# Low parts of weights by an accumulating SBUF-to-SBUF transfer instead of a VectorE subtraction

## The chip, the cores and the metric

The kernel runs on one core of a Trainium2 chip. The metric is device time in microseconds for one execution of the whole program, lower is better. The core has a matrix engine (PE, with its weight loads shown as PEld), a vector engine (DVE), a scalar engine (ACT), GpSimd (POOL), and a queue engine for transfers (SP). Each engine runs its own instructions in order and waits on semaphores that others raise. Transfers are issued from the queues of SP, ACT and POOL and carried by the core's 16 DMA engines; those of POOL are the ones that can add into their destination.

## The reference

One layer of a hybrid decoder trunk on a sequence of 2048 tokens with model width 1024, all in float32:

```python
mem_n = rmsnorm(mem, mem_norm_g)                       # 256 memory tokens
h = rmsnorm(x, mix_norm_g)
q, k, v, g, u = split(h @ w_in, [512, 1024, 1536, 2048])
y_ret = silu(g) * head_rmsnorm(retention(q, k, v, positions), ret_gn_g)   # 4 heads of 128
y_pool = pool_mixer(u, pool_w, pool_scale)             # 4 groups, windows 2, 4, 8, 16
x = x + concat([y_ret, y_pool]) @ w_out
x = x + cross_attn(rmsnorm(x, xa_norm_g), mem_n, xa_wq, xa_wkv, xa_wo)    # 4 heads of 256
x = x + conv_glu_ffn(rmsnorm(x, ffn_norm_g), w_up, conv_w, conv_b, w_down)  # hidden 2816
return rmsnorm(x, final_norm_g)
```

## The kernel before

**Numbers as pairs.** Every matrix product is made in three passes. A float32 operand is split into a high part, rounded to the matrix engine's fast format (`F32R`), and a low part, the rest. `passes` (L241 to L243) adds high by high, high by low and low by high into one PSUM bank. `split` (L230) makes a pair: ACT copies the source to the high part, rounding it (L233), and DVE subtracts the high part from the source to give the low part (a line of `tt`, L216). With a scale `g` the two lines are L236 (ACT) and L225 (DVE, through `stt`). The first two passes need only the weight's high part; the third, L243, is the first that reads its low part.

**Tiles and buffers.** The sequence is worked in two blocks of T = 1024 tokens, each in two halves of SUB = 512. Activations stand with features on the 128 partitions. `X` holds the pairs of the eight normed input tiles. `R` is five raw weight buffers of 128x1024 floats; `Q` is three buffers for pairs of 128x512. `Z` and `T` are work space for tiles of 1024 and 512. The tile framework gives each engine an order of its instructions by its own model of their times, and puts in the waits: a buffer is written again only when its last reader is done.

**A unit.** `unit` (L285) makes one 128x1024 tile of output features: SP loads 128x1024 weights into a raw buffer (`load_tile`, L305), `pairs` splits the two halves into two of the three pair buffers, and PE runs 24 matmuls for each half, 12 for each half of the tokens. Per block there are 12 units for the retention heads, 4 for the pooling groups (two of block 1's stand before its heads), 8 for the output projection (`wout_r` and `WPd`, loaded by L1536 and L1537) and 8 for the attention's output (`VWd`): 32, and 64 in all. A raw buffer goes back to SP when both its low parts are made.

**Around the units.** Before the first block, `folded_weights` multiplies the attention's matrices into `Md` (query by key) and `VWd` (value by output); its units of work go on between those of block 0's heads, and its splits are not touched by the change. `attention` (L822) loads `Md` in two halves by two head pairs: `load_m(0)` before its loop, `load_m(1)` during the first eight of its sixteen steps, one 128x1024 raw load (L835) and two splits each; the second half goes to a `Z` buffer. In the attention output of block 0 each unit is followed by `load_x` for block 1: two loads of x (L524), then ACT's L236 and a square (L355), DVE's L225 and a sum. SP's order there is: raw weights of five units on, then loads for the weight sums, then the two x tiles.

**POOL.** In the first 940 us POOL does two things. `weight_sums` forms sums of blocks of the feed-forward weights in DRAM (`Ud`, `Dd`): for each of 34 jobs SP loads four blocks (L913), and POOL adds others to them by accumulating transfers, two at once (L915, L916), then one that needs the first (L919), then one that needs the second (L922). The jobs are stepped between the quarters of a unit. `pool_group` has POOL copy 16 columns of halo (L630, L631) for each half of each group. Later come sums for the feed-forward stage (`sums_of`) and some of its low parts.

**Feed-forward.** From about 1190 us `run` works through `w_up` and `w_dn` in rounds with an order written out in the kernel; it has splits of its own (`Member`, `combining`) that the change leaves alone.

Of the kernel before, what the change touches and what calls it, by code (L numbers as in the profile page):

```python
# [8 lines left out]
F32 = mybir.dt.float32  # L9
F32R = mybir.dt.float32r  # L10
I32 = mybir.dt.int32
AF = mybir.ActivationFunctionType
ALU = mybir.AluOpType
# [8 lines left out]
SUB = 512  # L22
# [97 lines left out]
def trunk(ctx, tc, xT, memT, pos, w_qkgu, w_v, wkv, wqT, wo, wout_r, wout_p, poolT, w_up, w_dn, vecs, consts, outT):  # L120
    nc = tc.nc
    pe, act, dve, pool, sp = nc.tensor, nc.scalar, nc.vector, nc.gpsimd, nc.sync
# [15 lines left out]
    def new_z(dtype):  # L138
        return Arena(cp.tile([P, 8 * T + 4 * EDGE], dtype, tag="Z", name=nm("Z")), 0, 8, T)
# [58 lines left out]
    def mmps():  # L198
        return mmp.tile([P, SUB], F32, tag="mm", name=nm("mm"))
# [6 lines left out]
    def aux():  # L206
        if both[0] and next(turns_) % 3 == 2:
            return single()
        return auxp.tile([P, SUB], F32, tag="aux", name=nm("aux"))

    def small(n=4):
        t = smp.tile([P, 8], F32, tag="sm", name=nm("sm"))
        return t[:, :n]

    def tt(eng, out, a, b, op):
        return eng.tensor_tensor(out=out, in0=a, in1=b, op=op)  # L216

    def ts(eng, out, a, s1, op0, s2=None, op1=None):
        if op1 is None:
            eng.tensor_scalar(out=out, in0=a, scalar1=s1, scalar2=None, op0=op0)  # L220
        else:
            eng.tensor_scalar(out=out, in0=a, scalar1=s1, scalar2=s2, op0=op0, op1=op1)

    def stt(out, a, s, b, op0=ALU.mult, op1=ALU.add):
        dve.scalar_tensor_tensor(out=out, in0=a, scalar=s, in1=b, op0=op0, op1=op1)  # L225
# [4 lines left out]
    def split(src, hi, lo, g=None):  # L230

        if g is None:
            act.activation(hi, src, AF.Copy)  # L233
            tt(dve, lo, src, hi.bitcast(F32), ALU.subtract)
        else:
            act.activation(hi, src, AF.Identity, scale=g)  # L236
            stt(lo, src, g, hi.bitcast(F32), ALU.mult, ALU.subtract)

    def passes(ps, lhs, rhs, start, stop, more=False):
        (lh, ll), (rh, rl) = lhs, rhs  # L240
        pe.matmul(ps, lh, rh, start=start, stop=False, skip_group_check=more)  # L241
        pe.matmul(ps, lh, rl, start=False, stop=False, skip_group_check=more)  # L242
        pe.matmul(ps, ll, rh, start=False, stop=stop, skip_group_check=more)  # L243

    def new_raw():
        r = raws.take()
        r.free()
        return r.f

    def new_pair():  # L250
        r = prs.take()
        r.free()
        return r.r.rearrange("p (i n) -> p i n", i=2)

    def pairs(raw):

        out = []
        for h in range(2):
            r = raw[h] if isinstance(raw, list) else raw[:, h * SUB : (h + 1) * SUB]
            pr = new_pair()  # L260
            split(r, pr[:, 0], pr[:, 1])
            out.append(pr)
        return out

# [20 lines left out]
    def unit(raw, rhs, evac, order=range(4)):  # L285


        hs = pairs(raw)
        ps = [mmps() for _ in range(NS)]
        for h in range(2):  # L290
            for s in range(NS):
                for j, kk in enumerate(order):
                    k = 4 * h + kk
                    w = [hs[h][:, i, kk * P : (kk + 1) * P] for i in range(2)]
                    passes(ps[s], w, rhs(k, s), h + j == 0, h == 1 and j == 3)
                next(behind[0], None)
                quarter[0] += 1
                if not slow[0] or quarter[0] % 2:
                    next(under[0], None)
                if h == 1:  # L300
                    evac(s, ps[s])
# [520 lines left out]
    def attention(sums, beside, pace):  # L822


        scl, nscl = (smp.tile([P, 8], F32, tag="scl", name=nm("scl"), bufs=2) for _ in range(2))
        room = B.take(2 * KT)
        third = [Region(B, room.first + KT * i, KT) for i in range(2)] + [new_z(F32R).take(KT)]
        prob = [third[1], third[0]]

        def load_m(hp):  # L830

            out = mw[hp]
            for kp in range(KT // 2):
                raw = new_raw()
                fetched[0] = sp.dma_start(raw.rearrange("p (k n) -> p k n", k=2), Md[hp, 2 * kp : 2 * kp + 2].rearrange("k p n -> p k n"))  # L835
                if hp == 0 and kp == 0:

                    out += [(pr[:, 0], pr[:, 1]) for pr in pairs(raw)]
                    yield
                    continue  # L840
                for i in range(2):
                    u = third[2 * hp].r[:, (2 * kp + i) * T : (2 * kp + i + 1) * T]
                    split(raw[:, i * SUB : (i + 1) * SUB], u[:, :SUB], u[:, SUB:])
                    out.append((u[:, :SUB], u[:, SUB:]))
                yield

        def turn(pt, t, e):
            tp = aux()
            for j in range(4):
                pe.transpose(tp[:, j * P : (j + 1) * P], e.f[:, j * P : (j + 1) * P], ident)  # L850
            pt4 = pt.r.rearrange("p (i k t) -> p i k t", i=2, t=T)[:, :, :, t * P : (t + 1) * P]
            split(tp.rearrange("p (k t) -> p k t", k=4), pt4[:, 0], pt4[:, 1])
            e.free()

        mw = [[], []]
        for _ in load_m(0):
            pass
        more_m = load_m(1)
        late = []
        for i in range(2 * KT):  # L860
            hp, t = divmod(i, KT)
            ps = mmps()
            for k in range(KT):
                x2 = [X[:, 2 * k + j, t * P : (t + 1) * P] for j in range(2)]
                passes(ps, x2, mw[hp][k], k == 0, k == KT - 1)
            if i == 0:
                rn, _, _ = norm_tables(sums, wide=False)
                ts(dve, scl, rn, 1.0 / 16.0, ALU.mult)
                ts(dve, nscl, rn, -1.0 / 16.0, ALU.mult)
            mx, sm = small(2), small(2)  # L870
            dve.reduce_max(out=mx, in_=ps.rearrange("p (h m) -> p h m", h=2), axis=AX.X)
            ts(dve, mx, mx, nscl[:, t : t + 1], ALU.mult)
            e = TT.take()
            for j in range(2):
                act.activation(e.f[:, j * NMEM : (j + 1) * NMEM], ps[:, j * NMEM : (j + 1) * NMEM], AF.Exp,
                               bias=mx[:, j : j + 1], scale=scl[:, t : t + 1], accum_out=sm[:, j : j + 1])
            dve.reciprocal(sm, sm)
            for j in range(2):
                ej = e.f[:, j * NMEM : (j + 1) * NMEM]
                ts(dve, ej, ej, sm[:, j : j + 1], ALU.mult)  # L880
            if len(late) == 2:
                turn(*late.pop(0))
            late.append((prob[hp], t, e))
            for _ in range(pace):
                next(under[0], None)
            if i < KT - 2:
                next(more_m, None)
            else:
                for _ in range(pace):
                    next(beside, None)  # L890

        def end():
            for one in late:
                yield turn(*one)

        return prob, end()
# [129 lines left out]
    class Up(Member):  # L1026
# [15 lines left out]
        def evac(self, i, ps):  # L1042
            if i == 0:
                self.gate = self.place()
            elif i == 1:
                self.val = self.place()
            which, q, how = ((0, 0, 0), (1, 1, 0), (0, 1, 0), (0, 0, 1), (1, 1, 1), (0, 1, 1), (1, 0, 0))[i]
            d = body(self.val if which else self.gate)[:, q * SUB : (q + 1) * SUB]
            if how:
                tt(dve, d, d, ps, ALU.add)  # L1050
            else:
                act.activation(d, ps, AF.Copy)
            if i > 4:
                pending.extend(self.conv(i - 5))
# [365 lines left out]
    def norm_tables(s_acc, wide=True, late=False):  # L1420

        rn = rows_norm(s_acc)
        rb, last = [], None
        if wide:
            rb = [TT.take() for _ in range(NS)]
            last = spread(rn, [r.f[:, :SUB] for r in rb], late=late)
        return rn, rb, last
# [71 lines left out]
    for b in range(NB):  # L1499
# [34 lines left out]
        for n in range(KT):  # L1534
            raw = new_raw()
# [32 lines left out]
        for n in range(KT):  # L1568
# [3 lines left out]
            def rhs(k, s):  # L1572
                at = (k % 4) * T + s * SUB
                return tuple(prob[k // 4].r[:, i * 4 * T + at : i * 4 * T + at + SUB] for i in range(2))
# [152 lines left out]
```

## Time and profile before

| what | value |
|---|---|
| median of 3 runs | 2506.76 us (2502.85 to 2508.31) |
| the profiled execution's own time | 2506.72 us |
| its span, first to last instruction | 2504.9 us |
| PE busy in it | 2442.7 us |
| mean granted PE clock | 0.992 |
| DVE, ACT, POOL busy | 1666.9, 1216.1, 652.4 us |

How to read it: the busy time of an engine leaves out instructions that only wait, branch or issue transfers, except that POOL's issues, which have a duration, are counted in POOL's. Matmuls overlap, so that one of 0.39 us follows the one before after some 0.23 us. A row of the timeline gives start and duration in microseconds, engine, line, operation, output and inputs by their names in the kernel, shape, and in square brackets how long the engine was idle before it and what ended that. "DMA share" is the mean busy share of the 16 DMA engines.

The stages by time: folded weights alone to about 80 us; heads of block 0 with the rest of the folded weights to about 340; its pools to 390; output projection to 470; attention to 576; attention output to 671; norms, two pools and values of block 1 to 740; its heads to 900 and pools to 933; output projection to 1017; attention to 1113; attention output to 1200; then the feed-forward part and the final norm.

### The profile page before, as it was taken

Reading aid. Unit: us, or ns where it says so; the run is one execution under the profiler, and the core shown is the slowest. Engines: PE = TensorE matmul, PEld = TensorE weight load, DVE = VectorE, ACT = ScalarE, POOL = GpSimd, SP = SyncE. Lnnn points to the kernel's source line nnn. Section 1 sums busy time; section 2 is a strip of 40 time slices with the busy share of each in tenths; the row PEclk is TensorE's granted clock in tenths of the full one; section 3 lists DMA queues with packets and bytes.
Section 4 is the critical chain, followed back from the end, with each engine's and each line's share of the span. In section 5 each row is a group of like instructions: output and inputs, shape, how many; then the busy total and the mean of one; then the engine's idle time right before and its main releaser. Section 6 shows DMA issues by size and latency. Waiting matters only on the chain.

```text
span 2504.9 us, 33172 instructions
## 1 busy us (share of the span) xinstructions
PE 2442.7 (98%) x11390; PEld 2037.7 (81%) x11390; DVE 1666.9 (67%) x2574; ACT 1216.1 (49%) x2163; POOL 652.4 (26%) x579
## 2 busy tenths in 40 slices
PE   6999999999999999999999999999999999999997
PEld 6888887788788888888887888878888887888885
DVE  8646566564635675574678776886677586867875
ACT  6333423343321223434654555665555576666663
POOL 1010122100121120030237352553335154222322
PEclk9999999999999999999999999999999999999998
DMA  8363888715766764366567564755556468768951
GB/s 318 89 168 110 244 191 233 234 40 181 227 152 145 159 158 149 111 221 220 167 205 270 166 203 153 236 192 165 160 160 213 136 220 287 250 185 280 346 164 68
DMA packets 257177, 474.28 MB, mean 189 GB/s; under 512 B 26864, under 2 KB 56176, under 8 KB 257008
## 3 DMA queue, kind: packets, MB, share of 16 engines
q1 hardware_dynamic: 212336, 408.18, 49.0%
q0 software_dynamic: 19584, 34.61, 8.9%
q10 hardware_dynamic: 25088, 29.37, 3.4%
q8 instruction: 89, 1.46, 0.2%
q14 instruction: 80, 0.66, 0.1%
HBM read 370.87 MB, written 170.39 MB: 216 GB/s over the span
## 4 chain that ended last, share of the span: by engine, by line
PE 78%; DMA 8%; DVE 6%; issue 3%; POOL 2%; ACT 2%; SPq 0%; POOLq 0%; ACTq 0%; DVEq 0%
PE mm L241 25%; PE mm L242 24%; PE mm L243 24%; POOL T L216 1%; DVE Z L216 1%; DMA T<-Xd 1%; DVE Z L225 1%; DVE G L216 1%; DMA T<-xT 1%; DVE Q L216 1%; DVE T L216 1%; DMA T<-Gd 1%; POOL Z L216 1%; PE aux L749 1%; DMA R<-VWd 0%
## 5 line engine op out<-in xcount | busy, mean ns | idle before, releaser
L241 PE MATMUL mm<-G,Q 128*128 128x512 f32 (+1 forms) x1888 | 728.1, 386 | 21.8 <-ACT Q L233 11.1
L243 PE MATMUL mm<-G,Q 128*128 128x512 f32 (+1 forms) x1888 | 725.9, 385 | 4.4 <-DVE Q L216 4.2
L242 PE MATMUL mm<-G,Q 128*128 128x512 f32 (+1 forms) x1888 | 725.7, 385 | 0.7 <-DVE G L216 0.7
L241 PE MATMUL mm<-G 128*128 128x512 f32 (+1 forms) x1380 | 532.1, 387 | 10.0 <-DVE Z L216 6.3
L242 PE MATMUL mm<-G 128*128 128x512 f32 (+1 forms) x1380 | 531.7, 386 | 0.0
L243 PE MATMUL mm<-G 128*128 128x512 f32 (+1 forms) x1380 | 531.1, 385 | 0.0
L241 PEld LDWEIGHTS mm<-G,Q 128*128 128x128 f32 x1888 | 357.8, 190 | 91.1 <-ACT Q L233 11.8
L243 PEld LDWEIGHTS mm<-G,Q 128*128 128x128 f32 x1888 | 357.7, 190 | 74.3 <-DVE Q L216 5.9
L242 PEld LDWEIGHTS mm<-G,Q 128*128 128x128 f32 x1888 | 358.0, 190 | 69.4 <-DVE G L216 1.6
L225 DVE SCALAR_TENSOR_TENSOR Z<-Z,vecs 128x1024 f32<-128x1024 f32 x176 | 276.3, 1572 | 153.5 <-ACT Z L1069 145.3
L241 PEld LDWEIGHTS mm<-G 128*128 128x128 f32 x1380 | 260.4, 189 | 64.5 <-DVE Z L216 8.0
L243 PEld LDWEIGHTS mm<-G 128*128 128x128 f32 x1380 | 260.2, 189 | 51.8
L242 PEld LDWEIGHTS mm<-G 128*128 128x128 f32 x1380 | 260.1, 188 | 51.5
L1006 ACT ACTIVATE G<-R 128x512 fp32r<-128x512 f32 (+1 forms) x272 | 166.5, 615 | 197.8 <-PE mm L242 178.6
L216 DVE TENSOR_TENSOR Z<-Z,mm 128x512 f32<-128x512 f32 x284 | 192.8, 679 | 78.2 <-PE mm L243 78.0
L216 DVE TENSOR_TENSOR Q<-R,Q 128x512 fp32r<-128x512 f32 x199 | 148.6, 748 | 143.4 <-ACT Q L233 138.9
L216 POOL TENSOR_TENSOR G<-R,G 128x512 fp32r<-128x512 f32 (+1 forms) x100 | 141.9, 1420 | 376.2 <-ACT G L1006 290.9
L233 ACT ACTIVATE Q<-R 128x512 fp32r<-128x512 f32 x150 | 93.8, 627 | 234.8 <-PE mm L242 187.3
L1006 ACT ACTIVATE Q<-R 128x512 fp32r<-128x512 f32 (+1 forms) x204 | 125.0, 613 | 90.9 <-PE mm L242 73.5
L216 DVE TENSOR_TENSOR G<-R,G 128x512 fp32r<-128x512 f32 (+1 forms) x168 | 131.5, 794 | 46.7 <-ACT G L233 38.0
L216 DVE TENSOR_TENSOR G<-T,G 128x512 fp32r<-128x512 f32 (+1 forms) x168 | 125.4, 758 | 53.9 <-ACT G L955 40.7
L940 ACT ACTIVATE aux<-R 128x512 f32<-128x512 f32 (+1 forms) x184 | 105.8, 576 | 95.8 <-DVE Q L216 52.9
(222 smaller groups left out, 2911.4 us busy)
## 6 DMA issues: line engine op xcount, KB each, us to landing
R<-Ud SPq DMA_DIRECT2D x176, 256.0 KB, 2.7
T<-Gd SPq DMA_DIRECT2D x168, 256.0 KB, 4.1
R<-w_up SPq DMA_DIRECT2D x132, 256.0 KB, 3.1
Gd<-Z SPq DMA_DIRECT2D x110, 256.0 KB, 2.4
Ud<-w_up SPq DMA_DIRECT2D x88, 256.0 KB, 5.9
R<-w_qkgu SPq DMA_DIRECT2D x32, 512.0 KB, 4.4
R<-Dd SPq DMA_DIRECT2D x64, 256.0 KB, 4.0
Gd<-T SPq DMA_DIRECT2D x56, 256.0 KB, 3.1
```

The lines of the kernel that those rows point to most:

```text
L216: return eng.tensor_tensor(out=out, in0=a, in1=b, op=op)
L225: dve.scalar_tensor_tensor(out=out, in0=a, scalar=s, in1=b, op0=op0, op1=op1)
L233: act.activation(hi, src, AF.Copy)
L241: pe.matmul(ps, lh, rh, start=start, stop=False, skip_group_check=more)
L242: pe.matmul(ps, lh, rl, start=False, stop=False, skip_group_check=more)
L243: pe.matmul(ps, ll, rh, start=False, stop=stop, skip_group_check=more)
L749: pe.matmul(col(self.kv, c), col(self.kn.f, c), self.ch(v, c, h * T), start=True, stop=True)
L940: act.activation(t, x, AF.Copy)
L1006: act.activation(p2[:, 0, :w], self.raw[i].f[:, :w], AF.Copy)
```

## The change

A second way to make a pair, `moved`: ACT writes the negated source, rounded, into the low part; ACT writes the high part as before; then an accumulating transfer from POOL's queue adds the unrounded source to the low part, from SBUF to SBUF. Rounding is the same for both signs, so that the low part becomes the source less its high part, as before. The transfer is 128 rows of 512 floats, 256 KB. It is used for the two pairs of every unit (128 in all) and for the second half of the folded query-key weights (16). The other splits stay on DVE: the folded weights', the x tiles', the residuals', the pooled and mixed inputs', the value weights', the probabilities' and the first half of the query-key weights.

```diff
+    def moved(src, hi, lo):
+
+        act.activation(lo, src, AF.Copy, scale=-1.0)
+        act.activation(hi, src, AF.Copy)
+        pool.dma_start(lo.bitcast(F32), src, accum_op=ALU.add)
+
-    def pairs(raw):
+    def pairs(raw, how=split):
 
         out = []
         for h in range(2):
             r = raw[h] if isinstance(raw, list) else raw[:, h * SUB : (h + 1) * SUB]
             pr = new_pair()
-            split(r, pr[:, 0], pr[:, 1])
+            how(r, pr[:, 0], pr[:, 1])
             out.append(pr)
         return out
...
     def unit(raw, rhs, evac, order=range(4)):
 
 
-        hs = pairs(raw)
+        hs = pairs(raw, moved)
...
                 for i in range(2):
                     u = third[2 * hp].r[:, (2 * kp + i) * T : (2 * kp + i + 1) * T]
-                    split(raw[:, i * SUB : (i + 1) * SUB], u[:, :SUB], u[:, SUB:])
+                    (moved if hp else split)(raw[:, i * SUB : (i + 1) * SUB], u[:, :SUB], u[:, SUB:])
                     out.append((u[:, :SUB], u[:, SUB:]))
```

The framework makes the engines' orders anew. In the changed order ACT still writes the high part of a pair in Q ahead of its low part; POOL's 144 new transfers stand between the steps of the weight sums and the halo copies; SP's reload of a raw buffer waits for the two transfers that read it. From the feed-forward stage on, the order on every engine is the same as before.

## The prediction

> **What bounds the kernel now.** I read the page first, then the table of busy time by stretch, PE's waits, and last the timelines of single engines. The page:
>
> ```profile
> span 2504.9 us, 33172 instructions
> PE 2442.7 (98%) x11390; PEld 2037.7 (81%) x11390; DVE 1666.9 (67%) x2574; ACT 1216.1 (49%) x2163; POOL 652.4 (26%) x579
> ```
>
> The stretches (each engine's busy time with its instruction count, granted clock, DMA share, GB/s):
>
> ```profile
> 80.00:1200.00 1120.00, 1106.72 (x5349) 926.88 (x5349) 653.49 (x1308) 382.31 (x812) 148.37 (x187) 1.00 0.60 169
> 340.00:403.00 63.00, 58.95 (x286) 48.62 (x285) 42.45 (x94) 13.16 (x35) 21.09 (x34) 1.00 0.85 192
> 403.00:470.00 67.00, 67.00 (x297) 55.50 (x296) 38.83 (x61) 28.23 (x50) 5.72 (x7) 1.00 0.72 225
> 576.00:671.00 95.00, 93.91 (x428) 77.94 (x427) 48.66 (x78) 38.43 (x68) 7.12 (x9) 1.00 0.67 206
> ```
>
> PE is the bound. The changed work runs in 80 to 1200 us, where PE is busy 1106.72 of 1120 us: 13.3 us is all that any gain there can be. PE's waits in that stretch say for what it stands (us, times, longest):
>
> ```profile
> PE aux L850 <- DVE T L220: 4.5, 2, 4.3
> PE mm L241 <- ACT G L233: 3.9, 2, 3.0
> PE aux L339 <- DVE G L216: 1.7, 1, 1.7
> PE aux L315 <- DVE T L216: 1.1, 1, 1.1
> ```
>
> None of them is a wait for the low part of a weight. DVE's load costs something only where it delays the norms, the turned probabilities and the mixed inputs.
>
> **What goes, what comes.** The instructions, from the views of the tiles Q and Z (ns: min/median/max):
>
> ```profile
> L216 DVE TENSOR_TENSOR Q<-R,Q x132: 675/687/1360, 79.9 to 1197.8; 128x512 fp32r<-128x512 f32 x132
> L216 DVE TENSOR_TENSOR Z<-R,Z x16: 682/686/693, 464.5 to 1025.3; 128x512 fp32r<-128x512 f32 x16
> L233 ACT ACTIVATE Q<-R x129: 614/632/648, 125.9 to 1185.2; 128x512 fp32r<-128x512 f32 x129
> ```
>
> There are 2 x 32 units of two pairs, 128 low parts in Q, and 16 in Z for the attention's second half. DVE loses 144 x 0.687 = 99 us, ACT gains 144 x 0.63 = 91 us, and POOL gains 144 issues. ACT goes from 382 to about 473 of 1120 us, far from full. In ACT's order the high part still stands ahead of the new copy, so the first two passes (L241, L242) are no later. The third (L243) now waits for a transfer. Nothing in this trace adds from SBUF to SBUF; the nearest rows are POOL's other accumulating transfers (KB each, median us from issue to landing):
>
> ```profile
> Ud<-w_up POOLq DMA_DIRECT2D x44, 256.0 KB, 7.4
> Ud<-Ud POOLq DMA_DIRECT2D x44, 256.0 KB, 6.1
> Dd<-Dd POOLq DMA_DIRECT2D x16, 256.0 KB, 4.6
> Hd<-T SPq DMA_DIRECT2D x49, 256.0 KB, 2.4
> q0 software_dynamic: 19584, 34.61, 8.9%
> ```
>
> I take 4.6 us where these sums don't run and 6.1 us where they do, since size and packets are the same. Low bound: SP's plain 256 KB store to Hd lands in 2.4 us; high bound 7.4 us. From the start of the high part to the low part landed that is two ACT steps (0.53 + 0.63), some 0.2 us of hand-over, and the transfer: L = 6.0 us quiet, 7.5 us busy (3.8 to 8.8), against some 1.4 us now.
>
> The Trainium skill's page "DMA: Bandwidth & Descriptors", section "Anatomy of one DMA — SWDGE (gpsimd) path", gives 2.0 us plus bytes over 436 GB/s, an estimate of 2.6 us here; by it L would be 4.0 us and the sum below about +4 us. The trace's own 4.6 to 7.4 us disagree, and I go by them.
>
> **Where it is hidden: the dense units.** One pair in the output projection of block 0: ACT writes the high part, DVE the low part, PE reads them first (ACT, DVE, PE timelines):
>
> ```profile
> 436.56 0.63 ACT L233 ACTIVATE Q<-R 128x512 fp32r<-128x512 f32 x1 [3.40 <-PE mm L242]
> 437.23 0.69 DVE L216 TENSOR_TENSOR Q<-R,Q 128x512 fp32r<-128x512 f32 x1 [3.25 <-ACT Q L233]
> 447.41 0.39 PE L241 MATMUL mm<-G,Q 128*128 128x512 f32 x1
> 447.86 0.39 PE L243 MATMUL mm<-G,Q 128*128 128x512 f32 x1
> ```
>
> ACT starts when PE lets the slot go, and PE wants the low part 11.3 us later, because three pairs rotate and PE spends 5.4 us on each. L is under that, so the 16 pairs of each output projection cost nothing; without this cover each would cost L - 11.3. The head units, with retention between their matmuls, leave as much or more. The 16 transfers for the attention land long before their half begins. Cost 0.
>
> **Where it isn't: the attention output of block 0, 594 to 671 us.** Here SP, ACT and DVE form a ring:
>
> ```profile
> 634.04 0.38 SPq L657 DMA_DIRECT2D R<-w_v  x1
> 636.69 2.31 SPq L524 DMA_DIRECT2D T<-xT  x2
> 643.30 0.72 ACT L236 ACTIVATE G<-T,vecs 128x512 fp32r<-128x512 f32 x1 [5.38 <-DMA T<-xT]
> 645.59 0.62 ACT L233 ACTIVATE Q<-R 128x512 fp32r<-128x512 f32 x1
> 646.60 0.68 DVE L216 TENSOR_TENSOR Q<-R,Q 128x512 fp32r<-128x512 f32 x1
> 647.31 0.38 SPq L657 DMA_DIRECT2D R<-w_v  x1
> 648.48 0.39 PE L243 MATMUL mm<-G,Q 128*128 128x512 f32 x1
> 658.10 0.38 SPq L657 DMA_DIRECT2D R<-w_v  x1
> ```
>
> SP can't reload a raw buffer before its low part is made; behind that load stand the x tiles of block 1; ACT waits for these (5.38 us) and only then makes the next high part. One turn is 13.3 us, then 10.8, the time of a unit on PE. The low part was ready at 647.28 and wanted at 648.48: 1.2 us to spare. The change puts L for the 1.7 us from 645.59 to 647.28, at 6.0 to 7.5 us some 4.3 to 5.8 us more a turn, and the buffer stays held for as long. In the changed order two things ease it: one L236 with its square (1.3 us) moves behind the pair in each turn, and one x tile moves ahead of its reload, which opens that turn. So 3 to 4.5 us a turn remain, for three closed turns some 11 us; the 1.2 us to spare and what the first of them still has in hand come off. I take +8 us; ends 2 (L at its low bound) and 18 (four turns, nothing off).
>
> **POOL's queue.** POOL runs in order, and each job of the weight sums (L915, L916, L919, L922) waits twice for its own landing:
>
> ```profile
> 352.08 0.62 ACT L233 ACTIVATE Q<-R 128x512 fp32r<-128x512 f32 x1
> 354.85 0.81 POOL L919 DMA_DIRECT2D Ud<-Ud  x1 [1.88 <-DMA Ud<-w_up]
> 363.78 0.81 POOL L922 DMA_DIRECT2D Ud<-Ud  x1 [7.79 <-DMA Ud<-Ud]
> 366.06 0.39 PE L243 MATMUL mm<-G,Q 128*128 128x512 f32 x1
> ```
>
> In the changed order the transfer of the pair written at 352.08 stands behind the L922 of 363.78 (7.79 us of waiting): issued at 364.3, landed at 364.3 + 6.1 = 370.4, wanted at 366.06. That is 4 us of PE. The phalo copies (L630, L631) and the next sums queue behind it in turn. A second such place follows at the start of the output projection, behind an L915; but there PE already waits for the mixed input (the 3.9 us of L241 above), and DVE comes to it some 2 us sooner, with three low parts fewer ahead (3 x 0.69). I take +3 us for 340 to 403 us (-3 to +8).
>
> **Pairs let go late.** After the pools of block 1, and in the attention output of block 1:
>
> ```profile
> 941.76 0.63 ACT L233 ACTIVATE Q<-R 128x512 fp32r<-128x512 f32 x1 [2.03 <-PE mm L242]
> 946.12 0.39 PE L243 MATMUL mm<-G,Q 128*128 128x512 f32 x1
> 1131.15 0.62 ACT L233 ACTIVATE Q<-R 128x512 fp32r<-128x512 f32 x1
> 1136.70 0.39 PE L243 MATMUL mm<-G,Q 128*128 128x512 f32 x1
> ```
>
> 4.4 us from high part to use against L = 6.0: +1.6, with its two neighbours +3 (0 to 6). 5.5 us against 6.0: +0.5, taken as +1 (0 to 4).
>
> **Sum.** 8 + 3 + 3 + 1 = +15 us, less 2 us for DVE's lighter queue at the 7.3 us of norm and turn waits (L850, L339, L315), which are mostly fixed chains: +13 us. The profiled execution took 2506.72 us around its 2504.9 us span, the median of the runs is 2506.76: 2519.7 us. What follows 1200 us keeps its order on every engine.
>
> **Rivals.** (a) Hidden anyway: L near 3.8 us. Then the ring pays 2 us a turn, which the easing of its order absorbs, and the late pairs fit; 0 to 5 us, some 2509. For: Dd<-Dd at 4.6 us is already near. Against: DMA share 0.67 to 0.85 there. Chance 0.20. (b) Faster: at the start of block 0's output projection the mixed input is split by DVE after its pool chain; with the low parts off DVE the 3.9 us wait of L241 goes, and the L850, L339 and L315 waits shrink by half (3.6): 7 us less, 2499. It decides only if the transfers stall PE by under 2 us in all, so with L under about 4.5 us in the ring. Chance 0.09. (c) The transfers crowd each other. q0's 8.9% of the span is 223 us of all sixteen DMA engines for 136 transfers (34 jobs of the sums, four each), so 1.64 us for each. Two per 10.8 us unit add 0.30 to a share of 0.72 (403 to 470 us) or 0.67: near 1. Landings then stretch over 10 us, the 11.3 us of cover go, and some 20 units lose 2 us each: 2547. Chance 0.14. (d) Each transfer waits for DVE: POOL's issues took 0.81 us in the rows above; a stretch of one or two DVE instructions (0.69 each) would add up to 1.4 us to L, 3 to 5 us to the sum: 2524. It lies in the forecast's range; chance 0.07.
>
> For (d) the Trainium skill's page "SBUF — State Buffer", section "SBUF: two separate sides", says that DVE in a two-port mode locks GpSimd out of writing descriptors (620 ns become 3100 ns). The 0.81 us beside a DVE busy for 42 of 63 us speak against it here.
>
> **How the numbers follow.** Forecast 0.50 (2512 to 2535), (d) 0.07, (c) 0.14, (a) 0.20, (b) 0.09. 0.2% is 5 us, about what a measurement of this kernel tells from no change. Slower: 0.50 + 0.07 + 0.14 = 0.71; faster: (b) and 0.01 of (a), 0.10; same: the rest of (a), 0.19. The range leaves out half of (b) and half of (c): 2500 to 2546.
>
> **What would show it.** DVE some 99 us less, ACT 91 more, q0 with 144 transfers more; new PE idle before L243 ended by a DMA Q<-R, most of it between 594 and 680 us; SP's wait before the raw reloads of L305 and L657 ended by that DMA; POOL's issues of them late behind L919 and L922. Wrong if these transfers land in under 4.5 us beside the sums, if PE's idle time stays on L241, or if the output projections (403 to 470, 946 to 1017 us) show waits.

## The result and the profile after

The changed kernel takes 2639.9 us (median of 5 runs, 2635.8 to 2644.1) against 2507.5 us before on the same chip: ratio 1.0533, 95% interval 1.0517 to 1.0550. It is slower, as forecast, but by 132 us where the sum said 13, far outside the stated 2500 to 2546 us. The profiled execution has a span of 2634.0 us, 129 us over the one of before.

The page of the kernel after, its first rows, then rows of its parts on groups, queues and transfers (in the group rows: busy time, mean ns, then idle time before them and what ended it):

```profile
span 2634.0 us, 33540 instructions
...
PE 2475.4 (94%) x11390; PEld 2054.8 (78%) x11390; DVE 1581.2 (60%) x2430; ACT 1287.1 (49%) x2305; POOL 776.6 (29%) x723
...
q0 software_dynamic: 40320, 72.37, 17.3%
...
L243 PE MATMUL mm<-G,Q 128*128 128x512 f32 (+1 forms) x1888 | 735.8, 391 | 90.5 <-DMA Q<-R 85.9
...
Q<-R POOLq DMA_DIRECT2D x128, 256.0 KB, 5.4
```

DVE has 144 instructions and 86 us less, ACT 142 instructions and 71 us more, POOL 144 issues more. PE makes the same 11390 matmuls, but is busy 32.7 us longer and idle some 96 us more. 85.9 us of idle time stand before the third pass, L243, and end with the landing of a carried low part.

Three stretches of the kernel after, at the same clock times as in the kernel before, so that the work in them has slipped by up to 100 us (columns as in the prediction, which read the first two):

```profile
340.00:403.00 63.00, 49.65 (x235) 41.28 (x235) 23.89 (x62) 14.98 (x39) 15.97 (x25) 0.89 0.82 172
403.00:470.00 67.00, 50.14 (x197) 39.71 (x196) 26.95 (x45) 18.64 (x33) 19.67 (x27) 0.87 0.90 212
933.00:1017.00 84.00, 66.68 (x328) 55.86 (x328) 34.19 (x76) 17.99 (x43) 21.49 (x27) 0.90 0.77 147
```

PE, busy 58.95, 67.00 and 83.14 us in them before, now has 49.65, 50.14 and 66.68, and the granted clock is no longer 1.00. Because the stages slip, I cut both traces at the same matmul instead (PE's order of groups is known from both programs): the length of each stage, and in brackets PE's idle time in it, in us. "No sums" and "sums behind" are two of the experiments below.

| stage | before | after | no sums | sums behind |
|---|---|---|---|---|
| heads of block 0 | 260.0 (1.0) | 267.2 (6.8) | 258.4 (0.0) | 260.0 (1.4) |
| its pools | 63.2 (4.1) | 94.4 (27.0) | 58.0 (0.0) | 58.3 (0.0) |
| its output projection | 66.9 (0.0) | 74.4 (5.1) | 66.9 (0.0) | 77.4 (7.5) |
| its attention | 105.9 (4.3) | 110.4 (5.1) | 107.7 (4.9) | 111.4 (8.9) |
| its attention output | 95.0 (1.1) | 108.5 (10.5) | 105.4 (10.2) | 105.7 (10.2) |
| norms, two pools, values of block 1 | 69.1 (1.7) | 75.5 (7.1) | 74.4 (5.8) | 73.6 (5.3) |
| heads of block 1 | 193.0 (0.0) | 229.2 (27.0) | 192.9 (0.0) | 192.9 (0.0) |
| its pools' end and output projection | 84.0 (0.9) | 100.3 (14.3) | 84.8 (1.0) | 100.9 (13.6) |
| its attention | 95.9 (0.0) | 95.9 (0.0) | 96.0 (0.0) | 100.3 (2.5) |
| its attention output | 87.2 (0.2) | 92.0 (4.0) | 93.2 (3.5) | 91.4 (3.6) |

What follows, some 1295 us, is the same within 2 us. Two stages make half of the loss: the pools of block 0 (+31) and the heads of block 1 (+36). The sums of the feed-forward's weights run in both, with 20 and 40 of their transfers; in block 0's attention output, with 9, the loss is some 13 us.

Where it hangs is seen in one turn of block 1's heads after, from the timelines of SP, ACT, POOL and PE (start, duration; in brackets the idle time before and what ended it). SP loads ahead, so its reloads here already bring the weights of the output projection (L1542, L1543). In this kernel ACT's L258 writes a high part and L257 the negated copy, L259 is the carried transfer; a sum's loads are L919, and its transfers L921, L922, L925 and L928:

```profile
976.45 0.61 ACT L258 ACTIVATE Q<-R 128x512 fp32r<-128x512 f32 x1
976.97 0.61 ACT L257 ACTIVATE Q<-R 128x512 fp32r<-128x512 f32 x1
977.71 0.83 POOL L925 DMA_DIRECT2D Dd<-Dd  x1 [1.74 <-DMA Dd<-w_dn]
983.30 0.81 POOL L928 DMA_DIRECT2D Dd<-Dd  x1 [4.76 <-DMA Dd<-Dd]
983.83 1.20 POOL L259 DMA_DIRECT2D Q<-R  x1
989.12 0.33 SPq L1543 DMA_DIRECT2D R<-WPd  x1
989.51 2.42 SPq L919 DMA_DIRECT2D Dd<-w_dn  x4
989.93 0.61 ACT L257 ACTIVATE Q<-R 128x512 fp32r<-128x512 f32 x1
993.27 0.83 POOL L921 DMA_DIRECT2D Dd<-w_dn  x1 [8.24 <-DMA Dd<-w_dn]
995.21 0.84 POOL L922 DMA_DIRECT2D Dd<-w_dn  x1 [1.11 <-DMA Dd<-w_dn]
995.74 1.23 POOL L259 DMA_DIRECT2D Q<-R  x1
998.69 0.83 POOL L925 DMA_DIRECT2D Dd<-Dd  x1 [1.72 <-DMA Dd<-w_dn]
1002.58 0.80 PE L243 MATMUL mm<-G,Q 128*128 128x512 f32 x1 [7.11 <-DMA Q<-R]
1004.19 0.81 POOL L928 DMA_DIRECT2D Dd<-Dd  x1 [4.66 <-DMA Dd<-Dd]
1004.72 1.20 POOL L259 DMA_DIRECT2D Q<-R  x1
1009.58 0.33 SPq L1543 DMA_DIRECT2D R<-WPd  x1
```

Copies and transfers stand in the same order on their engines, so that they can be matched one by one over the whole run. The transfer issued at 995.74, for which PE stood 7.11 us, belongs to the copy of 976.97. That copy was ready at 977.6; its transfer stood 18.2 us in POOL's queue, behind L925, L928, the transfer of the pair before (983.83), L921 and L922. L921 alone waited 8.24 us for the sum's loads (L919). These were issued at 989.51, right behind SP's reload of a raw buffer (L1543), which itself had waited until the transfer of 983.83 had landed. The next pair, whose copy was ready at 990.5, had its transfer at 1004.72, behind L925 and L928, which waited for the sum's own landings; and SP's next reload of this kind, at 1009.58, came when that had landed. So a turn closes over POOL, SP, the sum's loads and POOL again: from one reload of this kind to the next it takes 20.5 us.

### The profile page after: what moved, and what is told of

Its sections match the earlier page's. It is cut to its first block, busy times and chain, and to the rows that moved or that the text cites. A ratio compares the mean times of both kernels' runs of the same rounds, so it can differ in the third digit from the quotient of the medians.

```text
span 2634.0 us, 33540 instructions
## 1 busy us (share of the span) xinstructions
PE 2475.4 (94%) x11390; PEld 2054.8 (78%) x11390; DVE 1581.2 (60%) x2430; ACT 1287.1 (49%) x2305; POOL 776.6 (29%) x723
## 3 DMA queue, kind: packets, MB, share of 16 engines
q8 instruction: 89, 1.46, 0.2%
## 4 chain that ended last, share of the span: by engine, by line
PE 47%; DMA 7%; issue 3%; DVE 3%; POOL 2%; ACT 1%; SPq 0%; POOLq 0%; ACTq 0%; DVEq 0%
PE mm L243 15%; PE mm L241 15%; PE mm L242 15%; DMA Q<-R 1%; DMA T<-Gd 1%; POOL T L216 1%; DMA Dd<-w_dn 1%; DVE Z L225 1%; DVE G L216 1%; DMA R<-Dd 1%; DVE Z L216 1%; DMA T<-Xd 1%; POOL Z L216 0%; DMA Dd<-Dd 0%; DMA T<-Hd 0%
## 5 line engine op out<-in xcount | busy, mean ns | idle before, releaser
L243 PE MATMUL mm<-G,Q 128*128 128x512 f32 (+1 forms) x1888 | 735.8, 391 | 90.5 <-DMA Q<-R 85.9
L241 PE MATMUL mm<-G,Q 128*128 128x512 f32 (+1 forms) x1888 | 735.1, 390 | 19.9 <-ACT Q L233 11.7
L242 PE MATMUL mm<-G,Q 128*128 128x512 f32 (+1 forms) x1888 | 731.1, 388 | 0.0
L243 PE MATMUL mm<-G 128*128 128x512 f32 (+1 forms) x1380 | 532.0, 386 | 0.0
L243 PEld LDWEIGHTS mm<-G,Q 128*128 128x128 f32 x1888 | 362.1, 192 | 172.3 <-DMA Q<-R 97.5
L241 PEld LDWEIGHTS mm<-G,Q 128*128 128x128 f32 x1888 | 362.5, 192 | 89.3 <-ACT Q L233 12.3
L242 PEld LDWEIGHTS mm<-G,Q 128*128 128x128 f32 x1888 | 362.1, 192 | 70.2 <-DVE G L216 0.4
L243 PEld LDWEIGHTS mm<-G 128*128 128x128 f32 x1380 | 260.6, 189 | 52.0
L259 POOL DMA_DIRECT2D Q<-R x128 | 128.7, 1041 | 449.7 <-ACT Q L257 430.7
L216 DVE TENSOR_TENSOR Z<-Z,mm 128x512 f32<-128x512 f32 x284 | 193.0, 680 | 86.9 <-PE mm L243 86.7
L258 ACT ACTIVATE Q<-R 128x512 fp32r<-128x512 f32 x128 | 80.5, 629 | 200.5 <-PE mm L242 155.6
L946 ACT ACTIVATE aux<-R 128x512 f32<-128x512 f32 (+1 forms) x184 | 106.2, 578 | 105.9 <-DVE Q L216 65.2
```

The source lines that it names most:

```text
L259: pool.dma_start(lo.bitcast(F32), src, accum_op=ALU.add)
L946: act.activation(t, x, AF.Copy)
```

## The experiments

**1. DVE adds instead of the transfer.** ACT's new copies stay.

```diff
-        pool.dma_start(lo.bitcast(F32), src, accum_op=ALU.add)
+        tt(dve, lo, src, lo.bitcast(F32), ALU.add)
```

> The low part is the negated rounded copy by ACT plus the source, added by DVE instead of the transfer: ACT has the work of the changed kernel, POOL and the DMA queues that of the kernel before. Theory (the loss of 132 us comes from where the transfers stand in POOL's queue, behind the weight sums, closed to a ring by SP's reloads): 2505 to 2515 us. Rival (ACT's 144 further copies, in order with everything else on ACT, make the loss): over 2580 us.

Measured 2505.1 us, ratio 1.0003 (0.9992 to 1.0015). ACT's 144 copies and the order they make cost nothing; the loss is in the transfer and where it stands.

**2. POOL subtracts.** The low part on POOL as a tensor subtraction, at the place of the transfer, with neither copy nor transfer.

```diff
-        act.activation(lo, src, AF.Copy, scale=-1.0)
         act.activation(hi, src, AF.Copy)
-        pool.dma_start(lo.bitcast(F32), src, accum_op=ALU.add)
+        tt(pool, lo, src, hi.bitcast(F32), ALU.subtract)
```

> The low part is made by one POOL subtraction (source less high part, as DVE did) where the transfer stood: no ACT copy, no transfer, the same queue behind the weight sums. Theory (POOL's order): still slow, but a step of some 1.4 us stands where a landing of 5 to 7 us stood, so the ring of about 21 us a unit shrinks to about 17: 2525 to 2580 us, with PE's waits before L243 ended by POOL Q. Rival (the landing time of the transfers, or their crowding on the DMA engines): 2505 to 2515 us.

Measured 2547.4 us, ratio 1.0173 (1.0150 to 1.0196). PE's waits in it (us, times, longest):

```profile
PE mm L243 <- POOL Q L216: 17.5, 8, 4.8
PE aux L320 <- DVE T L216: 10.5, 2, 7.5
```

With no new transfer at all, a low part that has to pass through POOL's queue makes the kernel 42 us slower. The subtraction itself takes 1.46 us on POOL in the median, far under the cover of 11.3 us that the prediction found; a place in that queue costs by itself. The second row is no wait for a low part, and its cause was not followed.

**3. The sums' steps apart.** Each step of a sum was written one job later, so that nothing in POOL's queue would wait.

```diff
...
+        made = [steps(job) for job in jobs]
+        for j in range(len(made) + 3):
+            for back, rest in enumerate((1, 2, 2, 0)):
+                if 0 <= j - back < len(made):
+                    made[j - back][back]()
+                for _ in range(rest):
+                    yield
```

> All 144 transfers stay; the steps of the weight sums are spread so that each POOL transfer of a job comes one job after what it waits for (loads of one job, first additions of the job before it, second of the one before that, and so on). Bytes and transfers are the same. Theory (waiting in POOL's queue): most of the loss goes, 2510 to 2540 us, with POOL's waits before the sums' transfers near zero. Rival (transfers crowd each other, or the raw buffers are held too long even without POOL's waits): over 2590 us.

Measured 2642.4 us, ratio 1.0551 (1.0531 to 1.0571). It tells nothing: the framework orders each engine's work anew, and POOL's order in this kernel is that of the changed kernel, instruction by instruction. An order has to be asked for; experiments 6 and 7 do that.

**4. Late stages only.** Carried from block 1's output projection on (the last 32 pairs and the eight of the attention).

```diff
-        hs = pairs(raw, moved)
+        hs = pairs(raw, moved if quiet[0] else split)
...
+        quiet[0] = b == 1
```

> The transfer only from the output projection of block 1 on, where no weight sums run: 32 pairs of units and 8 of the attention, the other 104 low parts back on DVE. Theory: 2503 to 2515 us, as the transfers land in under 4 us there and the pairs have 11 us. Rival (the transfer as such costs PE time in dense units): 16 units at 2 us or more, 2540 us and above.

Measured 2520.6 us, ratio 1.0067 (1.0048 to 1.0087): above what was expected. The expectation took it that no sums run there; the last of them still do, to 941 us. The pools' end and output projection took 98.4 us in place of 84.0, nearly all by one wait. POOL's timeline there, and PE's waits for carried parts in the whole run (us, times, longest):

```profile
927.71 0.83 POOL L921 DMA_DIRECT2D Dd<-w_dn  x1 [6.42 <-DMA Dd<-w_dn]
929.82 0.84 POOL L922 DMA_DIRECT2D Dd<-w_dn  x1 [1.28 <-DMA Dd<-w_dn]
930.36 0.51 POOL L637 COPY phalo<-T 128x16 f32<-128x16 f32 x1
935.62 0.82 POOL L925 DMA_DIRECT2D Dd<-Dd  x1 [4.75 <-DMA Dd<-w_dn]
936.19 1.16 POOL L259 DMA_DIRECT2D Q<-R  x1
```
```profile
PE mm L243 <- DMA Q<-R: 14.2, 4, 11.0
```

The copy for that transfer was ready at 925.1; the transfer was issued at 936.2, 11 us later, behind three transfers of one sum that waited. One such place cost 11 us of PE.

**5. Without the sums' transfers.** POOL's four transfers of each job left out, the loads by SP kept; once with the low parts carried, once with the kernel before as the control.

```diff
             yield
-            pool.dma_start(d[2], a22, accum_op=ALU.add, max_dma_last_dim=2048)
-            pool.dma_start(d[0], a21, accum_op=ALU.add, max_dma_last_dim=2048)
             yield
             yield
-            pool.dma_start(d[1], d[2], accum_op=ALU.add, max_dma_last_dim=2048)
             yield
             yield
-            pool.dma_start(d[3], d[1], accum_op=ALU.add, max_dma_last_dim=2048)
```

> Low parts carried by transfers everywhere, as in the changed kernel; the four accumulating transfers of each of the feed-forward's weight sums, which stand in POOL's queue, are left out (their loads by SP stay), so the sums are not formed. Theory (a unit's transfer stands in POOL's queue behind a sum's transfer that waits for its load or for the one before it, and the reload on SP behind the unit's transfer): the idle time before the units' matrix products goes from about 85 us to under 25, the time to 2505-2535 us. Rival (what costs is the carried low part itself: its issue on POOL, its flight of 3 to 8 us, the reload that waits for it): the idle time stays over 60 us and the time over 2580 us. In this run the sums' share of the DMA traffic is gone too, so a time of the first kind does not yet tell waiting from traffic; the next kernel does.

> The kernel before (low parts by VectorE) with the sums' four transfers left out, loads kept, so the sums are not formed: what they cost where no unit's low part stands in POOL's queue. Both theories: nearly nothing, 2498-2508 us, so that what the run without sums gains on the changed kernel comes from the two standing in one queue. If it falls below 2495 us, the sums' traffic by itself costs something.

Carried: 2523.2 us, ratio 1.0064 (1.0042 to 1.0086). Control: 2496.5 us, ratio 0.9954 (0.9938 to 0.9971). Without the sums the carried low parts cost 27 us, with them 132. In the table the heads, the pools and both output projections lose nothing any more, and the rest lies in block 0's attention and attention output, the norms, and block 1's attention output: 7.6, 11.6, 7.4 and 5.2 us over the control, whose stages took 100.1, 93.8, 67.0 and 88.0 us. The control was a miss by little: the sums cost the kernel before 11 us too.

**6. The sums behind the carried parts.** All traffic stays; steps one job apart as in experiment 3, and each ordered behind the latest carried transfer.

```diff
-        pool.dma_start(lo.bitcast(F32), src, accum_op=ALU.add)
+        carried[0] = pool.dma_start(lo.bitcast(F32), src, accum_op=ALU.add)
...
+            def first():
+                with tc.issue_after(carried[0].ins):
+                    pool.dma_start(d[2], a22, accum_op=ALU.add, max_dma_last_dim=2048)
+                    pool.dma_start(d[0], a21, accum_op=ALU.add, max_dma_last_dim=2048)
...
```

> Low parts carried everywhere, and every load and transfer of the sums kept, so the traffic is that of the changed kernel. Each sum's first transfers are put one job after its loads, its second and third one job later each, and each is ordered behind the latest transfer of a low part, which holds in POOL's queue this time. Theory (waits in POOL's queue): POOL no longer waits 250 us at the sums' first transfers but under 100, and the time is 2510-2550 us. Rival (traffic: transfers of both kinds slow each other in flight): the time stays over 2600 us, since all transfers are still there. Between 2550 and 2600 both would have a share.

Measured 2560.7 us, ratio 1.0210 (1.0187 to 1.0233). 79 of the 132 us are back, with every transfer in place; the pools of block 0 and the heads of block 1 lose nothing. What stays is largest in the output projections. POOL's timeline in the second of them, ahead of a wait of 9.36 us on PE (here L261 is the carried transfer, and L928, L929, L933 and L937 are the sums'):

```profile
971.55 0.88 POOL L261 DMA_DIRECT2D Q<-R  x1 [14.34 <-ACT Q L259]
972.10 1.22 POOL L933 DMA_DIRECT2D Dd<-Dd  x1
972.63 1.53 POOL L937 DMA_DIRECT2D Dd<-Dd  x1
973.17 1.85 POOL L928 DMA_DIRECT2D Dd<-w_dn  x1
973.69 2.17 POOL L929 DMA_DIRECT2D Dd<-w_dn  x1
974.78 1.99 POOL L261 DMA_DIRECT2D Q<-R  x1
975.37 2.27 POOL L933 DMA_DIRECT2D Dd<-Dd  x1
978.52 0.85 POOL L937 DMA_DIRECT2D Dd<-Dd  x1 [0.88 <-DMA Dd<-Dd]
979.11 1.18 POOL L261 DMA_DIRECT2D Q<-R  x1
981.73 0.86 POOL L261 DMA_DIRECT2D Q<-R  x1 [1.44 <-ACT Q L259]
```
```profile
991.54 0.79 PE L243 MATMUL mm<-G,Q 128*128 128x512 f32 x1 [9.36 <-DMA Q<-R]
```

Here the sums hold nothing up for long: the carried transfer of 979.11 was issued 3.2 us after its copy was ready. But ten transfers are sent in 10 us, the DMA share is 1.03 from 971.5 to 982 us and 1.10 from there to 991.5 (a packet is counted where it starts, so that this can pass 1), and the landings draw out: 3.9 us for the first, 12.4 us for the one of 979.11, for which PE stands until 991.5. So the crowd in flight has a share too, but the smaller one. That this flight is the cause of all that stays in the output projections was not tried by itself.

**7. The order alone.** The steps stay in their jobs; only the `issue_after` is added.

```diff
+            with tc.issue_after(carried[0].ins):
+                pool.dma_start(d[2], a22, accum_op=ALU.add, max_dma_last_dim=2048)
+                pool.dma_start(d[0], a21, accum_op=ALU.add, max_dma_last_dim=2048)
...
```

> Low parts carried everywhere; the sums' steps stay in their jobs (no step comes a job later), but each of their transfers is ordered behind the latest transfer of a low part. So the order in POOL's queue is that of the kernel which lost least with the sums in place, while a sum's first transfer still follows its own loads at once. Theory (a closed turn: the odd half's landing, the reload on SP, the sum's loads behind it, POOL waiting for them, the next unit's transfers behind that): the order alone does not open the turn, POOL still waits over 150 us for loads, and the time is 2570-2630 us. Rival (the order alone is what costs, a unit's transfer standing behind transfers of the sum that could have gone later): the time is that of the kernel with both, 2550-2570 us.

Measured 2564.6 us, ratio 1.0242 (1.0226 to 1.0258). My theory fell here: I had held that POOL must wait for the loads for as long as a step follows them at once. POOL's waits at the sums' steps, first after, then in this kernel, where the sums' transfers are L924, L925, L929 and L933 (its largest):

```profile
POOL Ud L921 <- DMA Ud<-w_up: 153.1, 20, 31.2
POOL Dd L921 <- DMA Dd<-w_dn: 88.6, 12, 10.2
POOL Ud L928 <- DMA Ud<-Ud: 81.1, 17, 8.4
POOL Ud L925 <- DMA Ud<-w_up: 56.6, 15, 7.5
```
```profile
POOL Ud L929 <- DMA Ud<-w_up: 36.6, 7, 8.8
POOL Ud L933 <- DMA Ud<-Ud: 31.8, 8, 8.4
POOL Dd L933 <- DMA Dd<-Dd: 30.8, 6, 8.4
POOL Dd L929 <- DMA Dd<-w_dn: 22.7, 6, 4.9
```

After, POOL waited 242 us at the first transfer of the jobs. With the carried transfers ahead the loads have landed by the time POOL comes to it, and that wait is gone. The steps that wait for the sums' own landings (L929 and L933) still wait 122 us in these rows, and yet the kernel is within 4 us of that of experiment 6, where nearly all of these waits are gone. What counts is not how long POOL waits but whether a unit's transfer stands behind it. (The framework moved a few instructions of the other engines too; of SP's 1447 transfers 16 stand elsewhere.) The kernel before says the same; POOL's waits at a job's first transfer there, 470 us with little behind them:

```profile
POOL Ud L915 <- DMA Ud<-w_up: 384.8, 16, 109.8
POOL Dd L915 <- DMA Dd<-w_dn: 85.1, 11, 27.6
```

**8. The same for the kernel before**, to look for a version faster than both: low parts by DVE, sums' steps apart and behind the pools' halo copies.

```diff
-            pool.tensor_copy(phalo[:, g], u.f[:, SUB : SUB + 16])
+            edge[0] = pool.tensor_copy(phalo[:, g], u.f[:, SUB : SUB + 16])
...
+                with behind_edge():
+                    pool.dma_start(d[1], d[2], accum_op=ALU.add, max_dma_last_dim=2048)
```

> The kernel before, low parts by VectorE, with the sums' transfers one job behind their loads, the later steps one job further, and each ordered behind the latest halo copy of the pools. The kernel before without the sums' transfers was 11 us faster than with them, 5 us of it in the pools of block 0, where halo copies stand in POOL's queue behind transfers that wait. Theory (waits in POOL's queue): these 5 us come back and the time is 2496-2505 us, faster than both kernels. Rival (the 11 us are the sums' traffic beside the loads of the units): no change, 2503-2512 us.

Measured 2505.1 us, ratio 1.0002 (0.9993 to 1.0011): no change. The pools of block 0 fell from 63.2 to 58.0 us as the theory said, but block 0's attention, into which more of the sums now reach, took 113.0 us in place of 105.9. No kernel that still forms the sums beats the one before.

**9. One stage at a time.** Carried only in the attention output of block 0, and only in the heads of block 1.

```diff
...
         fetch_acc(0)
+        carry[0] = b == 0
         for n in range(KT):
...
+        carry[0] = False
...
-        hs = pairs(raw, moved)
+        hs = pairs(raw, moved if carry[0] else split)
```

For the heads the flag is set around their loop instead, for block 1. The attention's 16 pairs are made by DVE in both.

> Low parts carried in the attention output of block 0 alone (16 pairs), all others by VectorE; no step of the sums runs there. It is the ring that the prediction put at +8 us (2 to 18). Theory (the ring by itself): that stage is 10 to 13 us longer, as it was with and without the sums elsewhere, and the time is 2513-2522 us. Rival (the stage loses only because earlier stages end late): under 3 us there, 2504-2510 us.

> Low parts carried in the head units of block 1 alone (12 units), where the prediction put nothing, beside the sums' transfers as in the changed kernel. Theory (a unit's transfers stand in POOL's queue behind the sums', stage by stage and not by heirs of an earlier delay): that stage is 25 to 40 us longer and the time 2530-2548 us. Rival (the loss there is carried over from the stages before): under 10 us, 2506-2517 us.

The attention output alone: 2517.9 us, ratio 1.0053 (1.0037 to 1.0068), 12.5 us. That stage took 107.7 us in place of 95.0. PE's and SP's waits in it:

```profile
PE mm L243 <- DMA Q<-R: 8.5, 3, 3.1
```
```profile
SPq L311 <- DMA Q<-R: 41.8, 5, 12.4
SPq L663 <- DMA Q<-R: 23.3, 3, 11.9
```

The heads of block 1 alone: 2528.5 us, ratio 1.0095 (1.0076 to 1.0113), 23 us, a little under what the theory gave. That stage took 218.7 us in place of 193.0, all other stages what they took before within 6 us (block 0's attention, which carries nothing here, 100.1 us). So most of the 36 us arise in that stage, not from what went before. The time that a transfer stands in POOL's queue grows there from pair to pair (5.4, 9.3, 9.7, 13.4, 17.0 us), falls back to 0.4 us and grows again to 19.1 us, as a turn that closes on itself would make it.

## Why the prediction was wrong, step by step

**Right: what bounds, and the counts.** PE is the bound, nothing was to be gained, and the time rose as forecast, though for the most part by a term that had been put at nothing. And the instructions moved as counted (POOL 144 more, DVE 144 fewer; in time DVE 86 us less in place of 99, ACT 71 us more in place of 91). Most of PE's waits are on L243 and end with a transfer Q<-R.

**Right, in mechanism and nearly in size: the ring of the attention output of block 0.** It was put at +8 (2 to 18), with 3 to 4.5 us a turn for three closed turns. Carried alone, that stage took 12.7 us longer: three waits, 8.5 us together and 3.1 at most, with SP waiting for Q<-R before the reloads, as said. Eight of the sums' transfers do run there, against what the expectation said, but no carried one stood in POOL's queue for more than 2.1 us; and without any sums the stage is 11.6 us over its control. The rest, some 5 us of PE's busy time, is slower matmuls, below. The flight was taken as 4.6 us quiet; without the sums the median of those to Q is 4.2 us and the shortest 3.2, so the size of the transfer was not the mistake, and the Trainium skill's 2.6 us (page "DMA: Bandwidth & Descriptors", section "Anatomy of one DMA — SWDGE (gpsimd) path") was too low here as well.

**Wrong, and the step that failed: "Cost 0" for the dense units and the heads.** The cover of 11.3 us was held against L = 6.0 to 7.5 us, that is against the work of ACT and the flight. The time that a transfer stands in POOL's queue before it is issued was left out of L, although the next part of the prediction had found just that at one place. In the turn above, PE came to the low part 19 us after the high part was begun, so that the heads did leave more cover than 11.3 us, as the prediction said. But the transfer stood 18.2 us in the queue, and L was 26 us. In experiment 4 the queue took some 11 us. Of the 144 carried transfers after, 32 were issued more than 5 us after their copy was ready, the latest 19.4 us; without the sums there are none, and in experiments 6 and 7 two and three. Without the sums the cover is enough: 66.9 and 84.8 us in the output projections and 192.9 us in the heads, as before. With them these three stages lost 7.5, 16 and 36 us. The heads of block 0 lost another 7 by way of SP: PE waits there 6.4 us for ACT's L750, in the longer of two waits because ACT stood for a load (L431) that SP could issue only when a carried transfer had landed, after 10.8 us. I had named waits in the output projections as what would prove the prediction wrong; they came.

**Mis-sized: POOL's queue, +3 (-3 to +8).** Its mechanism was right, a pair's transfer behind a sum's step that waits. I looked at one stage, 340 to 403 us, and at one pair in it, and found 4 us; the stage lost 31. And it is no sum of single delays: SP's reload waits for the late transfer, the sum's loads stand behind the reload on SP, and POOL waits for those, so that the delay comes back in the next turn. Neither link by way of SP was in this part of the prediction, though it said that SP's reload waits for the transfers. How much of the 31 and 36 us the closed turn makes and how much is plain delay in one pass was not separated: experiment 7 opened both with one edit.

**Mis-sized: pairs let go late, +3 and +1.** Block 1's attention output lost 4.8 us, a little over its bound of 4. After the pools of block 1 the cost is nothing without the sums and 14 us with them: the queue again.

**Not in it: the norms, two pools and values of block 1** (+6), where PE waits 6.9 us for a result of DVE (L345), and block 0's attention (+4.5). Over the control both lose some 7.5 us without the sums too; their cause was not tried.

**The rivals.** (a) and (b) are out: no stage of the changed kernel is shorter than before, so that DVE's relief brought nothing that can be seen. (c), crowding, 2547 us, was nearest to the time and named a place that did lose, block 0's output projection, but it put the loss in flight. With the traffic in place and the order changed, 79 us went away; the rest with the sums present is at most 37 us (2560.7 less 2523.2), of which the sums cost 11 in the kernel before. (d) is out as a main cause: the issues' median was 0.86 to 0.89 us in the runs with and without sums, while the time differed by 117 us.

The 132 us, then: 79 for the order in POOL's queue (after less experiment 6), 37 for the sums beside the carried transfers, less the 11 that they cost anyway, and 27 for the carried transfers alone (experiment 5 less its control), of which the ring is some 12.

## What to carry to other kernels

When a step moves to another engine's queue, its latency is not its own duration but that of everything ahead of it in that queue, waits included; so list, for each place where it will stand, what the instruction ahead waits for, and follow the waits of those who need the result until they close or end. A queue full of long waits is harmless only as long as nobody else's work stands in it; POOL was busy for 29% of the span here and still the wrong place for the step. And after moving work, look at the order that the scheduler made, and pin what must not stand behind a wait: here that alone brought back 75 of 132 us.

## What the runs showed of the hardware

PE's long waits cost more than their length. Three stretches of the kernel after around the wait of 7.11 us (columns as above; the clock is the third from the end):

```profile
995.47:1002.58 7.11, 0.00 (x1) 0.01 (x1) 0.29 (x1) 0.56 (x2) 2.34 (x3) 0.72 0.92 139
1002.58:1005.20 2.62, 2.62 (x9) 2.13 (x9) 0.00 (x0) 0.00 (x0) 1.01 (x2) 0.50 0.40 113
1005.20:1007.50 2.30, 2.30 (x12) 1.90 (x11) 1.20 (x2) 0.64 (x1) 1.73 (x3) 0.95 0.82 98
```

For 2.6 us after the wait PE works at a granted clock of 0.50, and a matmul takes 0.43 us from start to start in place of 0.23. Between 80 and 1330 us after has 13 waits of about 3 us and more, before two, and the same matmuls kept PE busy 32.7 us longer. The 32.7 us are a quarter of the loss, and the prediction had no term for them. In experiment 9, 17.4 us of waiting made the heads of block 1 25.7 us longer. Short waits did not do this: in the attention output of block 0 without the sums, five waits of at most 2.6 us, 10.2 us together, left the clock at 1.00 and made the stage 10.4 us longer. The Trainium skill's page "TensorE: Matmul & The Clock Gate", section "Part 1: The HAM clock gate (the "warmup" mystery)", says that the clock halves after an idle window of some 3.4 us and comes back after a busy one; the trace agrees in kind, with stretches like the 2.6 us above.

A carried transfer of 256 KB landed in 3.2 us at the shortest and 4.2 in the median without the sums, 5.4 to 5.7 in the median beside them, and up to 17.1 us in the kernel of experiment 6. Its issue kept POOL for 0.86 to 0.89 us in the median.
